# Gate and branch products of a token-mixing layer: feature-major at 256 columns, or token-major at 512

## The chip, the cores and the metric

The kernel runs on one core of a Trainium2 chip. Five engines matter: TensorE (PE; its weight loads are listed as PEld), VectorE (DVE), ScalarE (ACT), GpSimd (POOL) and SyncE (SP), which issues the DMAs. The metric is the time of one execution on the device in microseconds (us), and the median of several runs is compared.

## The reference

A trunk of two layers over 256 tokens of width 1024, in float32. Each layer is a SwiGLU feed-forward block (width 2816) at half weight, a mixing sub-layer, and another such feed-forward block. Only the mixing sub-layer is touched:

```python
h = rms_norm(x, mix_pre_g[l])
z = h @ w_in[l]
q, k, v, u_s, v_s, g_a, g_b = jnp.split(z, IN_SPLIT_POINTS, axis=-1)
y_attn = sliding_window_attention(q, k, v, attn_sinks[l])     # 16 heads of 64, 2 KV heads, window 128
y_sgu = spatial_gating(gelu(u_s), gelu(v_s), ...)             # chunks of 128 tokens
merged = (sigmoid(g_a) * (y_attn @ w_attn_branch[l])
          + sigmoid(g_b) * (y_sgu @ w_sgu_branch[l]))
x = x + rms_norm(merged @ w_out[l], mix_post_g[l])
```

Four products of 256 x 1024 by 1024 x 1024 concern us: the two gates `g_b` and `g_a`, and the two branches `y_sgu @ w_sgu_branch` and `y_attn @ w_attn_branch`.

## The kernel before

**Precision.** Every product is made in float32r from operands split into a high part (a cast on ScalarE) and a low part (what the cast lost, a subtraction on VectorE). Each product is three matmuls: high x high, high x low and low x high.

**Weights.** All weights come as units of 128 x 1024 float32 (512 KB) in one fixed order, through the class `Stream`. SyncE loads a unit into one of 4 raw buffers (L119), ScalarE casts it to the high part (L138), VectorE subtracts to the low part (L152). High and low parts stand in a ring of 9 (RING); units are converted up to 7 ahead of the one in use (AHEAD). The call `st.upto(n)` puts the next conversions into the queues, and a conversion waits on its engine until its ring place is free.

**The order of the mixing sub-layer** (`Mix.middle`) is written out by hand. A *slot* is one unit's product; `now[0]` counts them. In slots 0 to 7 the kernel makes u, in 8 to 15 q, 16 to 23 gate b, 24 to 31 the sgu branch, 32 to 39 gate a, 40 to 47 the attention branch, and from 48 the first four units of the output projection (`project`, whose call of `behind` continues the count). Side work is booked at half-slots: (n, 0) is put into the queues ahead of the product of slot n, (n, 1) behind it. `go(gen, half)` runs a generator one step, and a `yield 3` books its next step three half-slots later. So the attention (`attend`), with its six calls started at the half-slots of ATTEND, the spatial gating (`gating`) and the reading out of finished sums are woven between the products. Every engine then works through its own queue strictly in this order.

**Feature-major products** (`pairs`, `feature_major`, L259 to L261). One unit holds all 1024 inputs of 128 output features. For each of 8 chunks of inputs, a 128 x 128 block of weights is stationary and 256 tokens move: 24 matmuls of 256 columns per unit, the output standing as features x tokens. Two units share a PSUM bank, which is read out (`evac`) behind the next unit's product. For both gates and the sgu branch ScalarE copies the bank to SBUF (L834). At half-slot (40, 1) the block `gates` puts four sigmoids of 128 x 1024 into ScalarE's queue (L877) and two products of gate b with the sgu branch into GpSimd's (L879). The attention branch is merged as it comes (`merge`): VectorE multiplies by gate a out of PSUM (L888), GpSimd adds the gated sgu branch (L889), and ScalarE and VectorE split the sum into high and low (L891, L893), already features x tokens, as the output projection wants its stationary operand.

**Token-major products** (`passes`, L252). The feed-forward blocks' first products, the products for v and k, and all output projections are made the other way round: 128 tokens of activations are stationary, and 512 columns of weights move.

PSUM has eight banks, handed out by `bank()`. Transposes are made by TensorE (`transpose4`, L217: four blocks of 128 x 128 into one bank; L761 inside the attention).

## Time and profile before

| | |
|---|---|
| median of 3 runs | 1185.3 us (1185.28 to 1186.32) |
| profiled execution | 1186.02 us, span on the core 1184.3 us |
| granted TensorE clock, mean | 0.999 |
| TensorE busy | 1173.2 us, 99% of the span |
| VectorE busy | 835.7 us, 71% |
| ScalarE busy | 679.5 us, 57% |
| GpSimd busy | 60.0 us, 5% |
| DMA | 220.90 MB, mean 187 GB/s |

How to read it: the span is the time from the first to the last instruction on the core. An engine's busy time is the sum of its instructions' times with overlaps counted once. Matmuls are pipelined, so one matmul's listed duration (its mean in the groups) is longer than the time until the next one starts, and a busy TensorE need not be TensorE at its peak. "Idle before" names what ended the idle time of an engine, and the list of waits sums this up by pairs of lines. In the profile's rows an operand goes by the name of its pool: `m` and `n` are the eight-chunk tiles of pools `m8` and `n8` (gates, branches, merged sums), `t` is a temporary, `xt` the normalized input, `wh` and `wl` the high and low parts of a weight unit, `raw` a unit as loaded, `mm` a PSUM bank.

### The profile page before, as it was taken

The numbers are of one execution on the slowest core, as the hardware profiler recorded it, in microseconds if no ns is written. First come the engines' busy times: TensorE is split into PE (matmuls) and PEld (weight loads), VectorE is DVE, ScalarE is ACT, GpSimd is POOL, SyncE is SP. The second block draws the span as 40 slices with busy tenths as digits, with TensorE's granted clock in tenths as the row PEclk, the third lists the DMA queues.
The fourth block names the chain that finished last, engine by engine and source line by source line (L and its number), as shares of the span: only waits on it lengthen the run. The fifth ranks groups of instructions, "written<-read, shape, count | busy, mean of one in ns | idle before, by whom it ended". The sixth has DMA issues, their size and how long they took to land.

```text
span 1184.3 us, 18405 instructions
## 1 busy us (share of the span) xinstructions
PE 1173.2 (99%) x7031; PEld 1044.3 (88%) x7031; DVE 835.7 (71%) x1423; ACT 679.5 (57%) x1143; POOL 60.0 (5%) x40
## 2 busy tenths in 40 slices
PE   9999999999999999999999999999999999999997
PEld 7888887999999788888888888889999998888886
DVE  7768748887775966766586676588867678676752
ACT  5657634656766555655455665455577664665551
POOL 0000000001113100000000000000021040000000
PEclk9999999999999999999999999999999999999999
DMA  7566774655456546558725667745554663566560
GB/s 249 180 247 223 235 240 138 197 169 175 138 171 196 185 132 210 192 192 261 223 98 189 231 194 247 217 140 179 189 163 132 199 194 121 178 203 198 196 203 36
DMA packets 61288, 220.90 MB, mean 187 GB/s; under 512 B 7056, under 2 KB 7056, under 8 KB 61200
## 3 DMA queue, kind: packets, MB, share of 16 engines
q1 hardware_dynamic: 60912, 219.46, 57.1%
q8 instruction: 55, 0.90, 0.3%
q14 instruction: 33, 0.27, 0.1%
q10 hardware_dynamic: 288, 0.27, 0.1%
HBM read 218.65 MB, written 1.05 MB: 186 GB/s over the span
## 4 chain that ended last, share of the span: by engine, by line
PE 94%; DVE 2%; DMA 2%; ACT 1%; issue 1%; SPq 0%; DVEq 0%; ACTq 0%
PE mm L272 33%; PE mm L252 33%; PE mm L259 8%; PE mm L260 8%; PE mm L261 8%; PE mm L217 1%; DMA raw<-in_ffn_w 1%; DMA raw<-in_w_in 1%; PE mm L761 1%; PE mm L725 1%; DVE wl L152 1%; PE mm L724 1%; PE mm L694 1%; PE mm L774 0%; PE mm L773 0%
## 5 line engine op out<-in xcount | busy, mean ns | idle before, releaser
L152 DVE TENSOR_TENSOR wl<-raw,wh 128x1024 fp32r<-128x1024 f32 x372 | 455.9, 1251 | 112.3 <-ACT wh L138 111.5
L138 ACT CAST wh<-raw 128x1024 fp32r<-128x1024 f32 x372 | 383.0, 1050 | 164.2 <-DMA raw<-in_ffn_w 77.3
L272 PE MATMUL mm<-xt,wh 128*128 128x512 f32 x1152 | 290.7, 393 | 0.9 <-DVE xt L955 0.7
L252 PE MATMUL mm<-wh,m 128*128 128x512 f32 x832 | 258.5, 390 | 0.0
L272 PEld LDWEIGHTS mm<-xt,wh 128*128 128x128 f32 x1152 | 207.3, 189 | 38.7 <-DVE xt L955 1.2
L252 PEld LDWEIGHTS mm<-wh,m 128*128 128x128 f32 x832 | 156.2, 188 | 32.0
L272 PEld LDWEIGHTS mm<-xt,wl 128*128 128x128 f32 x1152 | 157.1, 190 | 11.2
L252 PE MATMUL mm<-wl,m 128*128 128x512 f32 x416 | 161.9, 389 | 0.0
L272 PE MATMUL mm<-xt,wl 128*128 128x256 f32 x1152 | 160.6, 282 | 0.0
L259 PE MATMUL mm<-xt,wh 128*128 128x256 f32 x512 | 146.2, 285 | 0.0
L261 PE MATMUL mm<-xt,wl 128*128 128x256 f32 x512 | 144.8, 283 | 0.0
L260 PE MATMUL mm<-xt,wh 128*128 128x256 f32 x512 | 144.8, 283 | 0.0
L639 DVE TENSOR_TENSOR t<-mm,t 128x256 f32<-128x256 f32 x144 | 60.7, 422 | 96.0 <-ACT t L638 96.0
L260 PEld LDWEIGHTS mm<-xt,wh 128*128 128x128 f32 x512 | 98.2, 192 | 0.2
L259 PEld LDWEIGHTS mm<-xt,wh 128*128 128x128 f32 x512 | 98.1, 192 | 0.2
L261 PEld LDWEIGHTS mm<-xt,wl 128*128 128x128 f32 x512 | 98.1, 192 | 0.0
L252 PEld LDWEIGHTS mm<-wl,m 128*128 128x128 f32 x416 | 78.1, 188 | 16.0
L638 ACT COPY t<-mm 128x256 f32<-128x256 f32 x144 | 52.9, 368 | 45.7 <-PE mm L272 45.6
L259 PE MATMUL mm<-m,wh 128*128 128x256 f32 x256 | 72.5, 283 | 0.0
L260 PE MATMUL mm<-m,wh 128*128 128x256 f32 x256 | 72.4, 283 | 0.0
L261 PE MATMUL mm<-m,wl 128*128 128x256 f32 x256 | 72.4, 283 | 0.0
L641 ACT ACTIVATE t<-t 128x256 f32<-128x256 f32 x72 | 30.1, 418 | 72.8 <-DVE t L639 72.8
(156 smaller groups left out, 1326.6 us busy)
## 6 DMA issues: line engine op xcount, KB each, us to landing
raw<-in_ffn_w SPq DMA_DIRECT2D x264, 512.0 KB, 4.4
raw<-in_w_in SPq DMA_DIRECT2D x84, 512.0 KB, 4.2
raw<-in_w_sgu_branch SPq DMA_DIRECT2D x16, 512.0 KB, 3.7
raw<-in_w_attn_branch SPq DMA_DIRECT2D x16, 512.0 KB, 4.5
raw<-in_w_out SPq DMA_DIRECT2D x16, 512.0 KB, 4.5
gain<-in_ffn_post_g SPq DMA_DIRECT2D x4, 512.0 KB, 6.8
gain<-in_ffn_pre_g SPq DMA_DIRECT2D x3, 512.0 KB, 8.0
x<-in_x SPq DMA_DIRECT2D x4, 256.0 KB, 4.2
```

The lines of the kernel that those rows point to most:

```text
L138: nc.scalar.copy(h, self.raw[u])
L152: nc.vector.tensor_tensor(out=lo, in0=self.raw.pop(u), in1=f(h), op=ALU.subtract)
L217: nc.tensor.transpose(ps[:, k, :], src[:, (c0 + k) * P:(c0 + k + 1) * P], ident)
L252: nc.tensor.matmul(o, every[i][0], every[i][1], start=start and i == 0, stop=stop and i == 2)
L259: nc.tensor.matmul(o, wh[:, ks], ah[:, k, :], start=(k == 0), stop=False)
L260: nc.tensor.matmul(o, wh[:, ks], al[:, k, :], start=False, stop=False)
L261: nc.tensor.matmul(o, wl[:, ks], ah[:, k, :], start=False, stop=(k == KD - 1))
L272: nc.tensor.matmul(out_, w[:, k * P:(k + 1) * P], x, start=(i == 0), stop=(i == len(todo) - 1))
L638: nc.scalar.copy(y[:, half, :], o[half][:, S:2 * S])
L639: nc.vector.tensor_tensor(out=y[:, half, :], in0=o[half][:, 0:S], in1=y[:, half, :], op=ALU.add)
L641: nc.scalar.activation(y[:, 0, :], y[:, 0, :], AF.Silu)
L694: nc.tensor.matmul(ps[:, i, n, :], vs[:, n, (g + i) * P:(g + i + 1) * P], self.wt[:, g + i, :], start=True, stop=True)
```

## The change

Gates and branches become token-major. The helper `row_major` takes a unit that holds 256 inputs (two chunks) of 512 output features, and for each of two token tiles makes six matmuls of 512 columns: 12 per unit. Four units make a *quad*: its two banks (one per token tile) stay open over four units and are then complete for 512 features. `quads` replaces `pairs` for the four products, and reads out token tile 0 ahead of the next unit's product and tile 1 behind it. The host lays the four weight matrices out to suit (`by_half`); units keep their size and order.

Gate b is copied to SBUF as before, but its sigmoids, two of 128 x 1024, go into slots 31 and 33 (GATE), and its products with the sgu branch, four of 128 x 512 on GpSimd, follow one slot later each. Gate a's sigmoid is taken straight from PSUM when a bank is read out. The block `gates` is gone. The merge multiplies and adds as before, on 512 features of 128 tokens; then, four half-slots later, TensorE transposes the sum in four blocks, and ScalarE and VectorE split it into high and low out of PSUM.

```diff
+GATE = (31, 33)
...
+    def row_major(o, u, m, ah, al):
+        wh, wl = st[u]
+        for t in range(NT):
+            for i in range(2):
+                k, ws = 2 * m + i, slice(i * 512, (i + 1) * 512)
+                passes(o[t], ah[:, k, rows_of(t)], al[:, k, rows_of(t)], wh[:, ws], wl[:, ws], (0, 1, 2),
+                       k == 0, k == KD - 1)
+        st.done(u)
...
+            def quads(units, ah, al, evac):
+                for j in range(KD):
+                    def product():
+                        if j % 4 == 0:
+                            o[:] = [bank() for _ in range(NT)]
+                        row_major(o, units[j], j % 4, ah, al)
+                        return units[j]
+                    if j % 4 == 0:
+                        o = [None] * NT
+                    beside(product)
+                    if j % 4 == 3:
+                        for t in range(NT):
+                            half = 2 * now[0] + t
+                            at(divmod(half, 2), lambda h=j // 4, t=t, o=o[t], half=half: go(evac(h, t, o), half))
...
-            gb = new(n8, [P, KD, S], "n8")
-            pairs(self.gb, xth, xtl, lambda j, o: to(gb, j, o))
-            so = new(n8, [P, KD, S], "n8")
-            pairs(self.sg, self.ysh, self.ysl, lambda j, o: to(so, j, o))
-            ga = new(m8, [P, KD, S], "m8")
-            pairs(self.ga, xth, xtl, lambda j, o: to(ga, j, o))
-            def gates():
-                for gt in (gb, ga):
-                    for h in range(2):
-                        hs = slice(h * 4, h * 4 + 4)
-                        nc.scalar.activation(gt[:, hs, :], gt[:, hs, :], AF.Sigmoid)
-                        if gt is gb:
-                            nc.gpsimd.tensor_tensor(out=so[:, hs, :], in0=so[:, hs, :], in1=gb[:, hs, :],
-                                                    op=ALU.mult)
-            at((now[0], 1), gates)
+            def rows_to(dst, h, t, o):
+                nc.scalar.copy(dst[:, t, halves()[h]], o)
+                yield from ()
+            gb = new(n8, [P, NT, D], "n8")
+            quads(self.gb, xth, xtl, lambda h, t, o: rows_to(gb, h, t, o))
+            so = new(n8, [P, NT, D], "n8")
+            def gate_b(h):
+                b = halves()[h]
+                nc.scalar.activation(gb[:, :, b], gb[:, :, b], AF.Sigmoid)
+                yield 2
+                for t in range(NT):
+                    nc.gpsimd.tensor_tensor(out=so[:, t, b], in0=so[:, t, b], in1=gb[:, t, b], op=ALU.mult)
+            for h, slot in enumerate(GATE):
+                at((slot, 0), lambda h=h, slot=slot: go(gate_b(h), 2 * slot))
+            quads(self.sg, self.ysh, self.ysl, lambda h, t, o: rows_to(so, h, t, o))
+            ga = new(m8, [P, NT, D], "m8")
+            def gate_a(h, t, o):
+                nc.scalar.activation(ga[:, t, halves()[h]], o, AF.Sigmoid)
+                yield from ()
+            quads(self.ga, xth, xtl, gate_a)
...
-            def merge(j, o):
-                js = slice(j, j + 2)
-                y = new(t2, [P, 2, S], "t2")
-                nc.vector.tensor_tensor(out=y, in0=o, in1=ga[:, js, :], op=ALU.mult)
-                nc.gpsimd.tensor_tensor(out=y, in0=y, in1=so[:, js, :], op=ALU.add)
-                yield 2
-                nc.scalar.copy(self.mh[:, js, :], y)
+            def merge(h, t, o):
+                b = halves()[h]
+                y = new(t2, [P, 512], "t2")
+                nc.vector.tensor_tensor(out=y, in0=o, in1=ga[:, t, b], op=ALU.mult)
+                nc.gpsimd.tensor_tensor(out=y, in0=y, in1=so[:, t, b], op=ALU.add)
+                yield 4
+                at_ = (slice(None), slice(h * 4, h * 4 + 4), rows_of(t))
+                ps = transpose4(y, 0)
+                nc.scalar.copy(self.mh[at_], ps)
                 yield 1
-                nc.vector.tensor_tensor(out=self.ml[:, js, :], in0=y, in1=f(self.mh[:, js, :]), op=ALU.subtract)
-            pairs(self.at, self.yah, self.yal, merge)
+                nc.vector.tensor_tensor(out=self.ml[at_], in0=ps, in1=f(self.mh[at_]), op=ALU.subtract)
+            quads(self.at, self.yah, self.yal, merge)
```

The part that `pairs` and `quads` share, `beside`, runs the work booked at (n, 0), the product, the work booked at (n, 1) and then the weight conversions, in the same order as `pairs` did before.

## The prediction

> **What bounds the kernel now.** I began with the page's first part (busy time and share of each engine) and its fourth (the chain that ended last).

> ```profile
> PE 1173.2 (99%) x7031; PEld 1044.3 (88%) x7031; DVE 835.7 (71%) x1423; ACT 679.5 (57%) x1143; POOL 60.0 (5%) x40
> PE 94%; DVE 2%; DMA 2%; ACT 1%; issue 1%; SPq 0%; DVEq 0%; ACTq 0%
> PE mm L272 33%; PE mm L252 33%; PE mm L259 8%; PE mm L260 8%; PE mm L261 8%; PE mm L217 1%; DMA raw<-in_ffn_w 1%; DMA raw<-in_w_in 1%; PE mm L761 1%; PE mm L725 1%; DVE wl L152 1%; PE mm L724 1%; PE mm L694 1%; PE mm L774 0%; PE mm L773 0%
> ```

> TensorE holds 94% of the chain. The lines the change touches, L259 to L261, hold 24%. A busy TensorE can still hide waits, so I asked next for all that TensorE waited for (us in total, times, longest):

> ```profile
> PE mm L977 <- POOL ident masks.py:199: 1.4, 1, 1.4
> PE mm L217 <- DVE t L453: 0.9, 2, 0.6
> PE mm L272 <- DVE xt L955: 0.7, 1, 0.7
> PE mm L252 <- ACT m L138: 0.4, 2, 0.3
> ```

> That is 3.4 us, none of it in the mixing sub-layer's gates and branches. Third, busy time in stretches of the first layer that hold the sgu branch (307.0), gate a (336.4) and the attention branch (362.1), then the same attention-branch stretch in the second layer:

> ```profile
> 307.00:336.40 29.40, 29.40 (x241) 29.01 (x240) 22.56 (x46) 21.93 (x59) 3.79 (x2) 1.00 0.41 126
> 336.40:362.10 25.70, 25.70 (x210) 25.35 (x209) 18.07 (x23) 15.42 (x24) 1.90 (x1) 1.00 0.70 198
> 362.10:385.10 23.00, 23.00 (x194) 23.00 (x193) 13.87 (x13) 15.99 (x18) 9.13 (x4) 1.00 0.56 185
> 946.30:969.30 23.00, 23.00 (x194) 23.00 (x194) 14.08 (x13) 16.45 (x18) 9.14 (x4) 1.00 0.58 188
> ```

> Columns: length, then PE, PEld, DVE, ACT and POOL, granted clock, DMA share, GB/s. TensorE is never idle, its clock is full, and DVE and ACT have a quarter or more to spare. So this stage lasts as long as its matmuls take to stream, and what counts is their pitch (start to start), not the duration in the groups. The timeline of TensorE gives it at both edges of the attention branch; the chain gives the 512-column pitch in output projections:

> ```profile
> 362.13 0.28 PE L259 MATMUL mm<-m,wh 128*128 128x256 f32 x1
> ...
> 385.17 0.40 PE L252 MATMUL mm<-wh,m 128*128 128x512 f32 x1
> ```
> ```profile
> 385.33 21.11 PE mm L252 x93
> 430.51 0.44 PE mm L217 x4
> 604.77 0.87 PE mm L217 x8
> 1117.07 59.87 PE mm L252 x264
> ```

> Eight units of 24 matmuls fill 385.17 - 362.13 = 23.04 us: 0.1200 us for 256 columns. The last projection's 264 matmuls of 512 columns take 59.87 us: 0.2268 us; the one right behind this stage gives 21.11/93 = 0.2270. Twice 0.1200 is 0.2400, so a wide matmul saves 0.0132 us against two narrow ones. A transpose takes 0.44/4 or 0.87/8 = 0.109 us.

> **The change part by part.**

> *Wider matmuls.* Gate b, sgu branch, gate a, attention branch: 4 x 8 units per layer, 64 in all. Each goes from 24 x 0.1200 = 2.880 us to 12 x 0.2268 = 2.722 us, a gain of 0.158 us; 64 of them give 10.1 us. The new order (token rows stationary, weights moving, three passes) is just that of L252, so I take its pitch whole. Bounds: 0.2400 (no gain) on the one side; on the other the two rows differ by 0.0002, and as much again below the lower one is 0.2 us more gain over the 768 wide matmuls.

> [...]

> *Transposes back.* The merged rows must become feature-major for the output projection: 4 merges per layer of 4 transposes each, 32 in all. None of these was there before. 32 x 0.109 = 3.5 us, all on TensorE's path. Lower bound the same; upper bound the duration of one in the groups, 0.273 (first row below), 8.7 us, if they did not overlap.

> ```profile
> L217 PE MATMUL mm<-ident,t 128*128 128x128 f32 x112 | 15.9, 273 | 1.0 <-DVE t L453 0.9
> L888 DVE TENSOR_TENSOR t<-mm,m 128x512 f32<-128x512 f32 x8 | 5.5, 684 | 0.1
> L889 POOL TENSOR_TENSOR t<-t,n 128x512 f32<-128x512 f32 x8 | 17.4, 2170 | 26.9 <-DVE t L888 26.9
> L152 DVE TENSOR_TENSOR wl<-raw,wh 128x1024 fp32r<-128x1024 f32 x372 | 455.9, 1251 | 112.3 <-ACT wh L138 111.5
> L138 ACT CAST wh<-raw 128x1024 fp32r<-128x1024 f32 x372 | 383.0, 1050 | 164.2 <-DMA raw<-in_ffn_w 77.3
> 382.16 2.32 DVE L152 TENSOR_TENSOR wl<-raw,wh 128x1024 fp32r<-128x1024 f32 x1
> ```

> [...]

> *The new wait.* Those transposes need product (DVE), sum (POOL), then TensorE; before, TensorE waited for nothing of the merge until the projection. For token tile 0 the sums end half a unit before the quad does, and the transposes stand two units later: 1.36 + 2 x 2.72 = 6.8 us. The chain needs 0.68 + 2.17 = 2.85, and 5.2 with one of the slowest weight subtractions (2.32, quoted) ahead of the product on DVE. For tile 1 there are three units, 8.2 us, and at worst another 2.17 on POOL. Taken: no wait. Upper bound: what a stall of DVE adds, below. Behind waiting transposes all of TensorE would stand. The copy and subtraction behind them read PSUM instead of SBUF, same count; the projection reads tile 0's second half two units after its transposes.

> *Gates on ACT and POOL.* These rows are the old block of sigmoids and what it did:

> ```profile
> 362.95 1.28 ACT L877 ACT_TABLE_LOAD   x1
> 364.24 2.01 ACT L877 ACTIVATE n<-n 128x1024 f32<-128x1024 f32 x2
> 366.15 1.99 ACT L877 ACTIVATE m<-m 128x1024 f32<-128x1024 f32 x2
> ```
> ```profile
> 369.12 4.41 DVE L152 TENSOR_TENSOR wl<-raw,wh 128x1024 fp32r<-128x1024 f32 x3 [8.62 <-ACT wh L138]
> ```
> ```profile
> L834 ACT ACTIVATE m<-mm 128x512 f32<-128x512 f32 x8 | 4.8, 598 | 11.2 <-PE mm L261 11.2
> L879 POOL TENSOR_TENSOR n<-n,n 128x1024 f32<-128x1024 f32 x4 | 9.6, 2420 | 53.3 <-ACT n L877 53.3
> ```

> ACT spent 5.3 us in one piece and DVE then idled 8.62 us, yet TensorE was busy all 23.00 us: the converted weights ahead of it covered the hole. After, gate a's two sigmoids go, because each takes the place of its copy (0.6 us, L834); gate b's two stay, in slots 31 and 33, behind the last exponentials (slot 30), so one table load per layer as before. ACT loses 2 us per layer that were already covered: gain nothing. POOL's gate products go from 2 x 2.42 to 4 of half the size, between 1.2 and 2.17 each, at 5% use, behind the last softmax scaling in its queue: nothing. Behind ACT's moved sigmoids stand weight casts, which come 1.05 us later, or 2.3 with the table load, against an 8.62 us hole that cost nothing.

> *Supply.* Units come every 2.72 us, needing 1.05 on ACT and 1.25 on DVE. In the fullest stretch DVE's 22.56 us would fall in 29.40 - 8 x 0.16 = 28.1 us: 80%. No DMA moves or changes size; SP issues the same units in the same order. 512 KB in 2.72 us is 193 GB/s; a stretch above had 198 at a DMA share of 0.70. Nothing charged. PSUM: a quad holds two banks for four units (10.9 us) during attention. The trace does not show banks; if a new quad met one still being emptied, the price would be up to 1.7 us, from the rows

> ```profile
> 343.08 1.04 PE L761 MATMUL mm<-ident,t 128*128 128x128 f32 x8
> ```
> ```profile
> 344.39 1.29 DVE L170 TENSOR_TENSOR t<-mm,t 128x512 fp32r<-128x512 f32 x2 [2.82 <-ACT t L169]
> ```

> (transposes done at 343.95, their bank read out at 345.68). Counting banks in order of release I find one close case per layer, and its second tile is written 1.36 us later, so I take zero; the upper end is 3.4 us for both layers.

> **Sum.** The profiled execution took 1186.0 us (span 1184.3 and 1.7 around it). 1186.0 - 10.1 + 3.5 = 1179.4. The median of the three runs is 1185.3, 0.7 below that execution, so I predict 1185.3 - 6.6 = 1178.7, 0.56% less.

> **Rivals.**

> *The merge becomes a wait of TensorE (other side).* If the weight supply stalls DVE in the attention branch as it did at 369.12, the product queues behind the subtraction and the transposes stop everything. Margin for tile 0 is 6.8 - 2.85 = 3.9 us; a repeat of the 8.62 us hole would cost 4.7 us in each place it hits. Two such per layer would add 19 us; the kernel becomes slower by 0.2% (1187.7) from 9.0 us on. Against it: that hole came from the block of sigmoids, which is spread out. Waits of 4.2 to 9.0 us end in "same".

> *The pitch goes by columns.* If at this place 512 columns cost 0.2400, nothing is gained and the transposes remain: 1185.3 + 3.5 = 1188.8. [...] For it: nothing in the rows; the 93 and 264 matmuls above are against it.

> *Transposes at full length.* 8.7 us instead of 3.5: 1183.9, no change. The eight in 0.87 us speak against it.

> **How the numbers follow.** About 0.2% (2.4 us) can be told from no change: faster is below 1182.9, slower above 1187.7. Forecast, with small waits up to 2 us: 0.80, at 1177 to 1181. Waits of 2 to 4.2 us (banks or merge): 0.06, still faster. Waits of 4.2 to 9.0: 0.05, same; more: 0.03, slower. Pitch by columns: 0.03, slower. Long transposes: 0.03, same. So faster 0.86, same 0.08, slower 0.06. The range goes from 1176.8 (0.2 us of the pitch bound, 1.0 of spread between the runs, 1185.28 to 1186.32, and the 0.7 by which the profiled execution stands above their median) to 1182.6 (banks at 3.4 us and 0.5 of a merge's wait).

> **What would show it.** The stretch of the attention branch up to the projection falls from 23.04 to 21.8 us plus transposes; its matmuls stand 0.227 us apart; L217-like transposes number 32 more, 0.44 us for four; the list of TensorE's waits has no new entry for the transposes from POOL; ACT has one table load for sigmoids per layer, early, with no hole of 8 us on DVE at the branch. The prediction is wrong if TensorE shows waits on POOL's sum or on a bank, or if the pitch is 0.24.

## The result

| | before | after |
|---|---|---|
| median on the device | 1185.5 us (6 runs, 1184.88 to 1186.37) | 1179.1 us (6 runs, 1178.63 to 1180.49) |
| ratio | | 0.9945, 95% interval [0.9936, 0.9955] |
| span of the profiled execution | 1184.3 us | 1178.8 us |

The kernel became 6.4 us faster; 6.6 us had been predicted.

The page of the changed kernel, busy time and the chain that ended last:

```profile
PE 1167.2 (99%) x6295; PEld 1007.7 (85%) x6295; DVE 839.7 (71%) x1423; ACT 676.8 (57%) x1139; POOL 59.9 (5%) x44
PE 98%; DVE 1%; DMA 0%; ACT 0%; issue 0%; SPq 0%; DVEq 0%
PE mm L254 51%; PE mm L284 34%; PE mm L261 3%; PE mm L262 3%; PE mm L263 3%; PE mm L219 2%; PE mm L773 1%; PE mm L737 1%; PE mm L736 1%; PE mm L706 1%; DMA raw<-in_ffn_w 0%; PE mm L786 0%; PE mm L785 0%; DVE t L1079 0%; ACT xt L1003 0%; DVE xt L1006 0%
```

Lines have moved down a little: L254 is the token-major matmul (L252 before), L261 to L263 the feature-major ones, L219 the transposes, L284 the feed-forward pairs. TensorE has 6295 matmuls and transposes, 736 fewer: 768 fewer matmuls and 32 more transposes. The feature-major lines keep 3% each (u and q) of their 8% each; the rest went to L254. DVE, ACT and POOL do about as much as before.

All that TensorE waited for, after:

```profile
PE mm L254 <- ACT m L140: 1.9, 1, 1.9
PE mm L1028 <- POOL ident masks.py:199: 1.4, 1, 1.4
PE mm L284 <- DVE xt L1006: 0.7, 1, 0.7
```

All three lie in the first 52 us. There is no entry for the transposes of the merged sums (L219 waiting for POOL). The chain in the first layer, from the attention branch into the output projection (start, length, what):

```profile
354.98 20.86 PE mm L254 x92
375.83 0.44 PE mm L219 x4
376.27 2.78 PE mm L254 x12
```

The wide matmuls follow one another every 20.86/92 = 0.2267 us, four transposes take 0.44 us, and the 12 matmuls right behind them 2.78 instead of 2.72.

To compare kernels without the start, which varies, I read two marks from each chain: the start of the long feed-forward stretch in the first layer (480 matmuls) and that of the last one. Between them lie both mixing sub-layers. Before, then after:

```profile
50.76 83.80 PE mm L272 x480
...
1033.26 83.81 PE mm L272 x480
```
```profile
52.31 83.81 PE mm L284 x480
...
1027.74 83.81 PE mm L284 x480
```

That is 982.50 us before and 975.43 after: 7.1 us less. In this execution the changed kernel reached the first mark 1.55 us later. TensorE had waited 1.9 us for the first weights, and the granted clock (the column behind the five engines) had a mean of 0.91 in the first 11 us, where it was 1.00 before. Before, then after:

```profile
0.00:11.00 11.00, 9.14 (x44) 7.99 (x45) 5.00 (x7) 5.14 (x7) 2.56 (x12) 1.00 0.79 285
```
```profile
0.00:11.00 11.00, 7.66 (x36) 6.88 (x37) 3.81 (x5) 4.51 (x5) 2.56 (x12) 0.91 0.80 286
```

The start is untouched by the change; the span's 5.5 us are 7.1 less this 1.55.

### The profile page after: what moved, and what is told of

Read it like the earlier page. It is cut to its first block, busy times and chain, and to the rows that moved or that the text cites. A ratio compares the mean times of both kernels' runs of the same rounds, so it can differ in the third digit from the quotient of the medians.

```text
span 1178.8 us, 16939 instructions
## 1 busy us (share of the span) xinstructions
PE 1167.2 (99%) x6295; PEld 1007.7 (85%) x6295; DVE 839.7 (71%) x1423; ACT 676.8 (57%) x1139; POOL 59.9 (5%) x44
## 3 DMA queue, kind: packets, MB, share of 16 engines
HBM read 218.65 MB, written 1.05 MB: 186 GB/s over the span
## 4 chain that ended last, share of the span: by engine, by line
PE 98%; DVE 1%; DMA 0%; ACT 0%; issue 0%; SPq 0%; DVEq 0%
PE mm L254 51%; PE mm L284 34%; PE mm L261 3%; PE mm L262 3%; PE mm L263 3%; PE mm L219 2%; PE mm L773 1%; PE mm L737 1%; PE mm L736 1%; PE mm L706 1%; DMA raw<-in_ffn_w 0%; PE mm L786 0%; PE mm L785 0%; DVE t L1079 0%; ACT xt L1003 0%; DVE xt L1006 0%
## 5 line engine op out<-in xcount | busy, mean ns | idle before, releaser
L254 PE MATMUL mm<-wh,m 128*128 128x512 f32 x1088 | 341.7, 391 | 0.0
L284 PE MATMUL mm<-xt,wh 128*128 128x512 f32 x1152 | 290.5, 393 | 0.7 <-DVE xt L1006 0.7
L254 PEld LDWEIGHTS mm<-wh,m 128*128 128x128 f32 x1088 | 204.3, 188 | 41.9
L284 PEld LDWEIGHTS mm<-xt,wh 128*128 128x128 f32 x1152 | 207.2, 189 | 38.4 <-DVE xt L1006 1.2
L254 PE MATMUL mm<-wl,m 128*128 128x512 f32 x544 | 211.8, 389 | 0.0
L284 PEld LDWEIGHTS mm<-xt,wl 128*128 128x128 f32 x1152 | 157.1, 190 | 11.3
L284 PE MATMUL mm<-xt,wl 128*128 128x256 f32 x1152 | 160.6, 282 | 0.0
L254 PE MATMUL mm<-wh,xt 128*128 128x512 f32 (+1 forms) x480 | 144.1, 378 | 0.0
L254 PEld LDWEIGHTS mm<-wl,m 128*128 128x128 f32 x544 | 102.2, 188 | 20.6
L254 PEld LDWEIGHTS mm<-wh,xt 128*128 128x128 f32 x480 | 88.4, 188 | 16.0
L254 PE MATMUL mm<-wl,xt 128*128 128x512 f32 (+1 forms) x240 | 87.5, 375 | 0.0
L261 PE MATMUL mm<-xt,wh 128*128 128x256 f32 x256 | 73.3, 286 | 0.0
L263 PE MATMUL mm<-xt,wl 128*128 128x256 f32 x256 | 72.4, 283 | 0.0
L262 PE MATMUL mm<-xt,wh 128*128 128x256 f32 x256 | 72.4, 283 | 0.0
L254 PE MATMUL mm<-m,xt 128*128 128x512 f32 x216 | 54.5, 397 | 0.0
L254 PEld LDWEIGHTS mm<-wl,xt 128*128 128x128 f32 x240 | 45.2, 188 | 7.8
L764 POOL TENSOR_TENSOR t<-t,rd 128x1024 f32<-128x1024 f32 x12 | 26.0, 2170 | 506.4 <-DVE rd L763 488.7
```

The source lines that it names most:

```text
L254: nc.tensor.matmul(o, every[i][0], every[i][1], start=start and i == 0, stop=stop and i == 2)
L261: nc.tensor.matmul(o, wh[:, ks], ah[:, k, :], start=(k == 0), stop=False)
L262: nc.tensor.matmul(o, wh[:, ks], al[:, k, :], start=False, stop=False)
L263: nc.tensor.matmul(o, wl[:, ks], ah[:, k, :], start=False, stop=(k == KD - 1))
L284: nc.tensor.matmul(out_, w[:, k * P:(k + 1) * P], x, start=(i == 0), stop=(i == len(todo) - 1))
L764: nc.gpsimd.tensor_tensor(out=p, in0=p, in1=rd[:, :nh].unsqueeze(2).to_broadcast([P, nh, nk]), op=ALU.mult)
```

## The experiments

Two theories were tried against each other. *Pitch*: each matmul carries about 13 ns beside its columns (2 x 0.1200 - 0.2268 us), so halving the number of matmuls gains 10.1 us, the transposes take 3.5 of it back, and moving the sigmoids is worth nothing. *Rivals*: the gain is the orientation, or comes from the moved sigmoids; or the transposes are hidden. In the table the marks are those of the profiled executions; the ratios are to runs of the kernel before on the same chip. The marks also hold small waits that have nothing to do with the change, up to 1 us in all (see *Not in the sum* below).

| kernel | median us | ratio to before [95%] | between the marks | against after |
|---|---|---|---|---|
| before | 1185.5 | 1 | 982.50 | +7.07 |
| after | 1179.1 | 0.9945 [0.9936, 0.9955] | 975.43 | 0 |
| e1_width256 | 1189.4 | 1.0032 [1.002, 1.0045] | 985.30 | +9.87 |
| e2_noturn | 1176.1 | 0.9923 [0.9911, 0.9936] | 971.73 | -3.70 |
| e3_block | 1189.7 | 1.0029 [1.0017, 1.0042] | 984.81 | +9.38 |
| e4_before_spread | 1185.4 | 0.9996 [0.9987, 1.0005] | 981.50 | +6.07 |
| e5_block_late | 1183.2 | 0.9979 [0.997, 0.9988] | 979.74 | +4.31 |
| e6_block_b | 1179.7 | 0.9947 [0.9933, 0.9961] | 975.47 | +0.04 |
| e7_yield1 | 1184.3 | 0.9979 [0.9969, 0.999] | 978.41 | +2.98 |
| e8_yield2 | 1179.8 | 0.9946 [0.9934, 0.9959] | 975.64 | +0.21 |

**Width alone (e1_width256).**

```diff
-                passes(o[t], ah[:, k, rows_of(t)], al[:, k, rows_of(t)], wh[:, ws], wl[:, ws], (0, 1, 2),
-                       k == 0, k == KD - 1)
+                for c in range(2):
+                    cs = slice(i * 512 + c * 256, i * 512 + (c + 1) * 256)
+                    passes(o[t][:, c * 256:(c + 1) * 256], ah[:, k, rows_of(t)], al[:, k, rows_of(t)],
+                           wh[:, cs], wl[:, cs], (0, 1, 2), k == 0 and c == 0, k == KD - 1 and c == 1)
```

> Token-major as in the changed kernel, but every wide matmul split into two of 256 columns (24 per unit again, same stationary blocks, same banks, same results). Pitch theory (each matmul carries about 13 ns beside its columns, so only the halved number of matmuls gains): 64 units x 0.158 us come back, 1179.1 + 10.1 = 1189.2 us, that is slower than before by the 3.5 us of the transposes; the pitch in the stage reads 0.120. Rival (the gain is the orientation, activations stationary and weights moving): 1179 us.

Measured 1189.4 us. Its chain, one row inside a quad and the two marks:

```profile
51.62 83.80 PE mm L286 x480
...
334.11 5.75 PE mm L254 x48
...
1036.92 83.81 PE mm L286 x480
```

5.75/48 = 0.120 us: with the activations stationary, the bank layout and the schedule of the changed kernel, the narrow matmul has the old pitch again. The whole gain of 10 us, and more than the net result, comes back. So it is the number of matmuls, not the orientation. Each of them comes with a weight load of its own (PE and PEld have the same count, 6295 in the changed kernel), so the loads were halved with the matmuls; which of the two carries the 13 ns no run tells.

**The transposes (e2_noturn).**

```diff
-                ps = transpose4(y, 0)
+                ps = y.rearrange("p (a b) -> p a b", a=4)
```

> The 32 transposes of the merged sums are left out: the sums go to the output projection untransposed, so that part of the computation is changed. Pitch theory (a transpose costs its pitch of 0.109 us on TensorE's path): 1179.1 - 3.5 = 1175.6 us. If they are covered by other work: 1179.1. If each costs its listed duration of 0.27 us: 1170.4.

```profile
51.17 83.80 PE mm L284 x480
...
1022.90 83.81 PE mm L284 x480
```

Measured 1176.1 us, and 3.70 us less between the marks, against 3.5 expected. The transposes stand in the open on TensorE's path at about their pitch: 8 x 0.44 is 3.5 us, and the matmuls right behind them are a few hundredths late each time. They are neither hidden nor do they cost their listed 0.27 us each.

**The sigmoids in one block again (e3_block).** Gate a is copied, and all four sigmoids are put in one piece behind it (`gate_b` makes the sigmoid of one half of gate b and its two products):

```diff
-                yield 2
...
-            for h, slot in enumerate(GATE):
-                at((slot, 0), lambda h=h, slot=slot: go(gate_b(h), 2 * slot))
...
-                nc.scalar.activation(ga[:, t, halves()[h]], o, AF.Sigmoid)
+                nc.scalar.copy(ga[:, t, halves()[h]], o)
...
+            def gates():
+                for h in range(2):
+                    gate_b(h)
+                for h in range(2):
+                    b = halves()[h]
+                    nc.scalar.activation(ga[:, :, b], ga[:, :, b], AF.Sigmoid)
+            at((now[0], 1), gates)
```

> The changed kernel, but with the old block of four sigmoids of 128 x 1024 in one piece behind gate a (slot 40), gate a copied first. Pitch theory: the placing of the sigmoids is worth nothing, 1179.1 us within 1 us. Rival (moving the sigmoids gains, because the block holds up VectorE, and with the merge in token-major form TensorE now waits for its product and sum): the hole of 8 us on VectorE comes back just ahead of the first merges, tile 0's transposes wait 1 to 3 us per layer, 1181 to 1185 us.

Measured 1189.7 us: 10.6 us slower than the changed kernel, far past both expectations. TensorE's list of waits has a new first entry:

```profile
PE mm L219 <- POOL t L944: 5.9, 2, 3.1
```

The chain goes back from the first transposes, by way of the product and the weights, to the sigmoids:

```profile
363.25 1.04 ACT n L915
364.29 1.89 ACT m L933 x2
366.19 0.95 ACT wh L140
...
369.48 1.22 DVE wl L154
370.72 4.45 DMA raw<-in_w_out
375.25 1.06 ACT wh L140
...
377.59 0.70 DVE t L943
378.42 1.27 POOL t L944
379.74 0.66 PE mm L219 x4
380.40 4.36 PE mm L254 x12
```

Read it downwards. ScalarE makes sigmoids until 366.2, so the weight casts come late; the raw buffers come free late, so the next weights land late (370.72, 4.45 us); VectorE subtracts for those weights first (it stands idle for 0.84 us ahead of the subtraction of 376.33), and the merge's product waits behind them until 377.59. TensorE stands before the transposes for 3.1 us. Then there is a second price: the 12 matmuls behind take 4.36 us instead of 2.72. The granted clock in stretches of the same execution says why (again the column behind the five engines):

```profile
380.00:381.00 1.00, 1.00 (x8) 0.86 (x7) 1.00 (x2) 0.98 (x2) 1.00 (x1) 0.98 0.75 307
381.00:382.00 1.00, 1.00 (x4) 0.81 (x3) 1.00 (x1) 0.55 (x2) 0.91 (x1) 0.50 0.29 45
...
384.00:385.00 1.00, 1.00 (x8) 0.80 (x6) 0.73 (x1) 0.00 (x0) 0.00 (x0) 0.81 0.76 168
```

Behind the wait the clock was 0.50 for some 3.4 us (382 to 384 read 0.50 as well), and 4.36 - 2.72 = 1.6 us went there. The second layer, after a wait of 2.8 us:

```profile
965.30 1.11 PE mm L219 x4
966.42 3.57 PE mm L254 x12
```

Here the half clock took in the transposes too: 1.11 + 3.57 is 1.5 us more than 0.44 + 2.72. Two layers: 5.9 us of waits and about 3.2 us of clock are 9.1 of the 9.38 between the marks.

**The same move without the wide matmuls (e4_before_spread).** The kernel before, with only the sigmoids moved:

```diff
+            def gate_b(h):
+                hs = slice(h * 4, h * 4 + 4)
+                nc.scalar.activation(gb[:, hs, :], gb[:, hs, :], AF.Sigmoid)
+                yield 2
+                nc.gpsimd.tensor_tensor(out=so[:, hs, :], in0=so[:, hs, :], in1=gb[:, hs, :], op=ALU.mult)
...
+            for h, slot in enumerate((31, 33)):
+                at((slot, 0), lambda h=h, slot=slot: go(gate_b(h), 2 * slot))
...
-            pairs(self.ga, xth, xtl, lambda j, o: to(ga, j, o))
...
-            at((now[0], 1), gates)
+            pairs(self.ga, xth, xtl, lambda j, o: to(ga, j, o, AF.Sigmoid))
```

> The kernel before, feature-major, with only the sigmoids moved as in the change: gate b's in slots 31 and 33 with their products two half-slots later, gate a's straight from PSUM. Pitch theory: 1185.5 us, no change. Rival (part of the gain is that ScalarE does 2 us less per layer and VectorE has no 8 us hole): below 1184.

Measured 1185.4 us, ratio 0.9996 [0.9987, 1.0005]: no change that can be told, at most 1.0 us between the marks. The same block that costs 9 us in the token-major kernel costs nothing in the feature-major one: there TensorE's list of waits (in the prediction) has no entry for the merge.

**Is it the wait at the transposes? (e5_block_late)** The block as in e3_block, the first half's transposes one unit later:

```diff
-                yield 4
+                yield 4 if h else 6
```

> The kernel with the sigmoids in one block (1189.7 us), and the first half's transposes booked six half-slots behind the merge in place of four, that is one unit later on TensorE. If the block costs only through TensorE's wait at those transposes (3 us in each layer, and the half clock that follows such a wait), the loss goes: 1179 to 1181 us. Rival (the block costs by delaying the weights or the projection): stays near 1189.

Measured 1183.2 us; 6.5 of the 10.6 us came back by the medians and 5.1 of 9.4 between the marks, less than expected. What is left on TensorE's list:

```profile
PE mm L219 <- POOL t L944: 1.7, 2, 1.3
PE mm L254 <- DVE m L950: 0.8, 2, 0.5
PE mm L254 <- ACT m L948: 0.2, 1, 0.2
```

Waits at the transposes fell from 5.9 to 1.7 us, the longest 1.3, and the clock read 1.00 in every stretch from 376 to 390 us, around the wait in the first layer. But the merge is now so late that the projection's first matmuls wait for the split behind the transposes (L950, L948). These 2.7 us are most of the 4.31 left; about 1.6 us I could not place. Some of it goes with the waits themselves: the four transposes behind a wait take 0.66 us on the chain in e3_block, where they take 0.44 without one.

**Half the block (e6_block_b).** Gate a's sigmoids as in the change, only gate b's two sigmoids and their products back at slot 40.

```diff
-                yield 2
...
-            for h, slot in enumerate(GATE):
-                at((slot, 0), lambda h=h, slot=slot: go(gate_b(h), 2 * slot))
...
+            def gates():
+                for h in range(2):
+                    gate_b(h)
+            at((now[0], 1), gates)
```

> The changed kernel with gate b's two sigmoids and their products moved back to slot 40, gate a's straight from PSUM as in the change: a block of 3.4 us on ScalarE in place of 5.3. Merge-wait theory: the product comes 2 us earlier than with the whole block, the first transposes wait about 1 us per layer and the clock stays: 1181 to 1182 us. Rival (any block there costs the same): 1189.

Measured 1179.7 us, +0.04 us between the marks, and no wait for POOL on TensorE's list; 1 us of waits per layer had been expected. Its products on VectorE, the first sum on GpSimd and TensorE's first transposes:

```profile
373.79 1.29 DVE L940 TENSOR_TENSOR t<-mm,m 128x512 f32<-128x512 f32 x2
```
```profile
374.63 1.31 POOL L941 TENSOR_TENSOR t<-t,n 128x512 f32<-128x512 f32 x1 [5.98 <-DVE t L940]
```
```profile
376.13 0.60 PE L219 MATMUL mm<-ident,t 128*128 128x128 f32 x4
```

Counted from the first mark, the product starts 3.4 us earlier than in e3_block (373.79 - 52.62 against 377.59 - 53.05), where I had reckoned with the 2 us that ScalarE saves. Tile 0's sum is done at 374.63 + 1.31 = 375.94, 0.2 us before the transposes start. There is hardly any room left, but nothing is lost. So of the two moves of the sigmoids, gate a's is enough; where gate b's stand did not matter.

**How much room the transposes have (e7_yield1, e8_yield2).** The changed kernel with `yield 4` in `merge` made `yield 1` and `yield 2`.

> The changed kernel with the transposes booked one half-slot behind the merge in place of four: both token tiles' transposes stand one unit behind the quad. From its trace tile 0's sum is there just in time, tile 1's 1.2 to 1.3 us late, at four places: waits of 5 us in all on TensorE, each too short to lower the clock: 1184 us. Rival (the sums have more room than the trace shows): 1179.

> The changed kernel with the transposes booked two half-slots behind the merge: tile 0 one unit behind the quad, tile 1 two units. By the trace both sums are there in time by 0 to 1 us: 1179 to 1180 us. Rival (the changed kernel's place for them, one unit later, is needed): over 1181.

With 1: 1184.3 us, the time that was expected, but the profiled execution shows only two of the four waits, at the first half:

```profile
PE mm L219 <- POOL t L938: 2.6, 2, 1.4
```

2.6 us of waits and +2.98 between the marks there, against a median that is 5.2 us above the changed kernel's; that execution took 1182.9 us, and other runs went up to 1185.5. What the longer executions waited for was not traced, so the hit on 1184 is in part luck. With 2: 1179.8 us, +0.21, no wait for POOL. So two half-slots do, one does not; the change has a unit to spare at tile 0.

## Why the prediction was right, point by point

*The pitch.* Predicted 0.2268 us and 10.1 us gained; the chain shows 0.2267, and undoing the width alone costs 9.87 us between the marks. Of the ways against it, the pitch that goes by columns is out: by it a wide matmul would have taken 0.2400 us.

*The transposes.* Predicted 3.5 us, measured 3.7 between the marks. The difference fits the matmuls right behind: 2.78 us for 12 instead of 2.72 at four of the eight places.

*The new wait.* Predicted none, and there was none. Here are the products, the two sums (each from a window of its own) and the first transposes in the changed kernel (VectorE, GpSimd, TensorE):

```profile
369.25 1.23 DVE L154 TENSOR_TENSOR wl<-raw,wh 128x1024 fp32r<-128x1024 f32 x1 [0.85 <-ACT wh L140]
370.51 1.29 DVE L937 TENSOR_TENSOR t<-mm,m 128x512 f32<-128x512 f32 x2
371.71 2.00 DVE L154 TENSOR_TENSOR n<-raw,n 128x1024 fp32r<-128x1024 f32 x1
```
```profile
371.34 1.29 POOL L938 TENSOR_TENSOR t<-t,n 128x512 f32<-128x512 f32 x1 [26.39 <-DVE t L937]
372.59 2.28 POOL L938 TENSOR_TENSOR t<-t,n 128x512 f32<-128x512 f32 x1
```
```profile
375.67 0.60 PE L219 MATMUL mm<-ident,t 128*128 128x128 f32 x4
```

Tile 0's product did not start when its sums in PSUM were done, at about 369.0 (the quad ends 24 matmuls ahead of the transposes, tile 0 half a unit earlier), but behind a weight subtraction that had itself waited for its cast. Tile 0's sum was ready at 371.34 + 1.29 = 372.63, and its transposes started at 375.67. The margin was 3.0 us, not the 3.9 that I had worked out, though this sum took 1.29 us and not 2.17. The rival I set beside it, VectorE held up by ScalarE's block, is real: in e3_block it hit one place per layer, at 4.7 us each. That this equals the price I had named for a place is chance, for it is made up differently (3.1 of wait and 1.6 of clock in the first layer; the clock was not in the prediction). What kept it out was the very part that I costed at nothing.

*The sigmoids.* "Gain nothing" holds for the kernel before (e4_before_spread). As a part of this change it is wrong in one way: the cover that I named, converted weights ahead of TensorE, protects the weights' users alone. A merge that TensorE itself waits for is not covered by it: with both moves undone the kernel is slower than before (e3_block, ratio 1.0029). Undoing gate b's alone cost nothing (e6_block_b); gate a's alone was not undone. ScalarE after the change:

```profile
334.01 1.28 ACT L915 ACT_TABLE_LOAD   x1
335.30 1.06 ACT L915 ACTIVATE n<-n 128x1024 f32<-128x1024 f32 x1
...
340.98 1.06 ACT L915 ACTIVATE n<-n 128x1024 f32<-128x1024 f32 x1
...
348.11 1.07 ACT L926 ACTIVATE m<-mm 128x512 f32<-128x512 f32 x2
```

One table load, gate b's two sigmoids 5.7 us apart with weight casts between them, gate a's in place of its copies: no block is left.

*Supply and PSUM.* No new wait for a weight or a bank appears behind the start of the changed kernel, as predicted. (Two figures there were a little off and nothing hangs on them: the quoted transposes end at 343.08 + 1.04 = 344.12, so the price of a bank is 1.6 us, and VectorE had 23% to spare in the fullest stretch, not a quarter.)

*Not in the sum.* Between the marks 7.07 us went, 0.9 more than width and transposes account for (9.87 - 3.70 = 6.17). The traces place most of it ahead of the change. These are the first transposes in the two mixing sub-layers, before, then after:

```profile
194.29 0.63 PE mm L217 x4
...
778.51 0.63 PE mm L217 x4
```
```profile
195.30 0.44 PE mm L219 x4
...
775.93 0.63 PE mm L219 x4
```

From the long feed-forward stretch ahead of them (50.76 and 635.12 before, 52.31 and 632.84 after) it is 143.53 and 143.39 us to these before, 142.99 and 143.09 after: 0.84 us less. The 0.9 us that TensorE waited there for VectorE before (`PE mm L217 <- DVE t L453` in the prediction's list) are all but gone, in work that the change does not touch; such waits differ between the executions (0.5 us in e2_noturn, 0.4 in e4_before_spread). From these transposes to the next long stretch (449.54 and 1033.26 before, 446.88 and 1027.74 after) it is 255.25 + 254.75 us before and 251.58 + 251.81 after: 6.6 us less, as predicted. Counted the same way, width is worth 9.85 us and the transposes 3.75, so 0.5 us stay open; the second layer of the kernel before and both layers of e4_before_spread have 254.8, so they lie in the first layer of the one execution before.

## What to carry to other kernels

Count a TensorE-bound stage by the start-to-start pitch of its matmuls, taken from a run of many of the same width: here each matmul, with its weight load, carried 13 ns beside its columns, so 512-column matmuls beat pairs of 256 by 5.5%, enough to pay for transposes at 0.11 us each. When a change makes TensorE wait for a chain through other engines, look at what stands in those engines' queues ahead of it: a block on ScalarE that was free while TensorE waited only for weights cost 9 us once it stood ahead of the merge. A wait of TensorE of about 3 us cost more than itself here: 1.6 us more in the first layer, where the granted clock was 0.50 for 3.4 us behind it, and 1.5 in the second.

## What the runs showed of the hardware

```profile
380.95:381.00 0.05, 0.05 (x2) 0.05 (x1) 0.05 (x1) 0.05 (x2) 0.05 (x1) 0.56 0.20 82
964.60:964.70 0.10, 0.00 (x0) 0.00 (x0) 0.10 (x1) 0.10 (x1) 0.10 (x1) 0.68 2.63 246
```

In the first layer the stretches around the fall read 1.00 (376 to 380) and 0.50 (381 to 382). With the same step in both layers, an estimate from these means, the change came at 380.956 and 964.636 us. In the first layer the clock fell 1.2 us after TensorE had gone on, in the second while it still stood, 0.7 us before its transposes. So the fall had no fixed distance from the wait; what sets its moment no run shows.

The changed kernel has such a stretch at its start, behind the wait of 1.9 us for the first weights (TensorE went on at 8.49):

```profile
8.90:8.95 0.05, 0.05 (x2) 0.05 (x1) 0.05 (x1) 0.05 (x1) 0.00 (x0) 0.95 0.80 328
8.95:9.00 0.05, 0.05 (x2) 0.05 (x1) 0.05 (x1) 0.01 (x1) 0.00 (x0) 0.50 1.60 655
...
12.30:12.35 0.05, 0.05 (x2) 0.05 (x1) 0.05 (x1) 0.05 (x2) 0.00 (x0) 0.50 0.62 246
12.35:12.40 0.05, 0.05 (x1) 0.05 (x1) 0.05 (x1) 0.05 (x2) 0.00 (x0) 0.92 1.82 655
12.40:12.45 0.05, 0.05 (x1) 0.04 (x1) 0.05 (x1) 0.05 (x2) 0.00 (x0) 1.00 0.21 82
```

The clock was 0.50 from 8.945 to 12.358 us, for 3.41 us.

GpSimd's sum of 128 x 512 took 2.17 us (mean of eight) in the kernel before; after, the first of each pair took about 1.3 and the second 2.28. In the rows under *The new wait* VectorE's subtraction of 371.71 takes 2.00 us in place of 1.23, while GpSimd makes its two sums (371.34 to 374.87). No run varied this, so the cause is not shown.
